# A decoder trunk on one core: the first layer's modulation and norm, done by halves in another order

## The chip, the core and the metric

The kernel runs on one core of a Trainium2 chip. The metric is device time in microseconds (us) of one launch. Engines, as the profile names them: PE is TensorE (PEld its weight loads), DVE is VectorE, ACT is ScalarE, POOL is GpSimd, SP is SyncE, which issues the large DMA transfers here.

## The reference

A trunk of two layers over 256 tokens of width 1024, float32. Each layer has three sub-layers (a half-step SwiGLU feed-forward network, FFN; a mixer; a second FFN), each behind an RMSNorm that is modulated by a vector computed from `c`. What the change touches is the start: the modulation of the very first norm, that norm, and the first products of the first FFN.

```python
def rmsnorm(x, g):
    y = xf * lax.rsqrt(jnp.mean(xf * xf, axis=-1, keepdims=True) + EPS)
    return y * g
def modulated_norm(x, g, shift, scale):
    return rmsnorm(x, g) * (1 + scale) + shift
def swiglu(h, wg, wu, wd):
    return (jax.nn.silu(h @ wg) * (h @ wu)) @ wd
c_act = jax.nn.silu(c)
mod = (c_act @ w_ada[l] + b_ada[l]).reshape(b, N_MOD, 1, D_MODEL)
sh1, sc1, g1, sh2, sc2, g2, sh3, sc3, g3 = [mod[:, i] for i in range(N_MOD)]
h = modulated_norm(x, norm_g[l, 0], sh1, sc1)
x = x + 0.5 * g1 * swiglu(h, ffn_wg[l, 0], ffn_wu[l, 0], ffn_wd[l, 0])
```

## The kernel before

**Layout.** Activations lie transposed: eight tiles `xt[t]` of 128 features by 256 tokens. Weights come from memory in float32; each weight tile is split into a high part `wh` (ACT, L369) and a low part `wl` (DVE or POOL, L384), and each activation tile into `hi` and `lo`. A product is three matmuls, wh·hi, wl·hi and wh·lo, one after the other for every 128 features (`mm`, L306 to L317).

**The start.** SP loads `x`, then the columns of `w_ada` that give shift and scale. These come in two halves: half 0 for features 0 to 511, half 1 for features 512 to 1023, each as eight loads of 512 KB. One such load holds 128 of the 1024 rows of `w_ada` (every eighth), 512 scale and 512 shift columns; the code calls the k-th load row k. For a half, DVE adds up the eight rows, each times its value of silu(c), into one tile `acc0` (L159 for the first row, L161 for the others), and PE sums over the 128 partitions with eight matmuls against a column of ones (L1390). DVE adds the bias and makes the factor `gsc` and the shift (L1396, L1399).

Meanwhile PE transposes `x`, ACT copies the results to `xt` and squares them, POOL adds up the squares (L1487), PE sums them over partitions (L564), and the reciprocal root is computed by small operations, nearly all of them on POOL (L448 to L456). The result is spread over the partitions by PE (L582) into `rtile`; POOL multiplies `xt` by it (L590), and DVE, POOL and ACT make hi and lo of the normalized tiles (L609, L610, L614).

**The first products.** Before the second half of the normalized tiles exists, the FFN can begin on the first: `lead` makes units. A unit is two blocks of 128 FFN columns over one half of the features, 24 matmuls. Six unit pairs (`LEADS = 12` blocks of columns) run on half 0: five, then the products of half 1's modulation, then the sixth; then the same six run on half 1. After these the FFN goes on with whole columns (`plain`: one block, all features, also 24 matmuls).

**What sets the order.** The program order is written step by step (`Step`, `run`, `plan`): before a step's matmuls, `split_high` and `split_low` issue the splits of later steps up to a lead time. `hold` shifts this time for a step, and `LLO` names the engine of the low split in the units. At most `UBUF = 5` split weight tiles are live. Raw weights and the rows of `w_ada` share a ring of `RAWB = 8` buffers of 1 MB: a load waits until the buffer's last user is done, and SP issues in order, so a waiting load holds up all behind it. The rest of the modulation (128 rows) is added up by DVE in the background at a rate per step (`tick`, `MTICK`).

## Time and profile before

| | |
|---|---|
| time, median of 3 runs | 1019.17 us (1018.66 to 1019.98) |
| profiled execution | 1018.38 us, of which its span is 1016.6 us |
| busy in the span | PE 96%, DVE 79%, ACT 48%, POOL 4% |
| TensorE's clock over the span | 0.985 of full |

The span runs from the first to the last instruction. 96% is an average: the idle time and the time at the lower clock lie at the two ends, and the stretch from 0 to 89 us is the one to read closely. Matmul ends are modelled, so a row's duration covers one matmul's whole passage; the pace is the distance between starts.

### The profile page before, as it was taken

To read this page: it belongs to the slowest core of one execution; us is meant where nothing else is said; L and a number is where in the kernel's file an instruction comes from. 1 tells how busy PE (TensorE), PEld (TensorE's weight loads), DVE (VectorE), ACT (ScalarE), POOL (GpSimd) and SP (SyncE) were. 2 spreads that over 40 slices of the span, in tenths; PEclk is the share of its full clock that TensorE was granted. 3 is DMA by queue.
4 is the path that set the end of the run, shared out by engine and by line. 5 is a ranking of instruction groups with operands and counts; after the bars stand their busy time and mean duration, and the time that the engine had idled before them with its cause. 6 is when DMAs were issued, how large, how long until landed. Compare 5 with 4: busy or idle time off the path is not lost.

```text
span 1016.6 us, 17795 instructions
## 1 busy us (share of the span) xinstructions
PE 972.2 (96%) x7126; PEld 919.1 (90%) x7126; DVE 801.3 (79%) x1288; ACT 483.3 (48%) x841; POOL 45.7 (4%) x81
## 2 busy tenths in 40 slices
PE   3879999999999899999999999999999999999998
PEld 1879999889878799999889999988999999999986
DVE  4768888888988799999898988888688889555552
ACT  2435444444653555444555544444564456444441
POOL 6820000000000000000000000000000000000000
PEclk9779999999999899999999999999999999999999
DMA  9879998888617659998796899876645556645410
GB/s 356 307 268 321 332 312 282 284 295 309 224 43 250 231 176 366 323 372 308 277 329 227 260 336 318 301 242 201 208 165 191 183 167 210 204 157 168 144 52 22
DMA packets 183284, 247.05 MB, mean 243 GB/s; under 512 B 5968, under 2 KB 156548, under 8 KB 183200
## 3 DMA queue, kind: packets, MB, share of 16 engines
q1 hardware_dynamic: 182944, 245.78, 70.2%
q8 instruction: 56, 0.92, 0.3%
q14 instruction: 28, 0.23, 0.1%
q0 software_dynamic: 256, 0.12, 0.0%
HBM read 244.84 MB, written 1.05 MB: 242 GB/s over the span
## 4 chain that ended last, share of the span: by engine, by line
PE 69%; DVE 21%; ACT 4%; issue 2%; DMA 2%; POOL 1%; SPq 0%; ACTq 0%; DVEq 0%; POOLq 0%
PE pu L315 45%; PE acc L326 11%; DVE wl L384 7%; PE acc L327 6%; DVE acc L161 4%; PE acc L315 3%; DVE nh L600 1%; DVE xp L605 1%; ACT wh L369 1%; PE acc L995 1%; DMA raw<-in_ffn_wg_dram 1%; DVE tx L628 1%; DMA raw<-in_ffn_wu_dram 1%; PE pu L1390 1%; POOL ssum L1487 1%
## 5 line engine op out<-in xcount | busy, mean ns | idle before, releaser
L315 PE MATMUL pu<-xp,wh 128*128 128x256 f32 (+1 forms) x3008 | 547.4, 283 | 6.2 <-DVE xp L530 2.6
L315 PEld LDWEIGHTS pu<-xp,wh 128*128 128x128 f32 x3008 | 467.0, 190 | 8.4 <-DVE xp L530 3.1
L315 PE MATMUL pu<-xp,wl 128*128 128x256 f32 (+1 forms) x1504 | 423.7, 282 | 0.7 <-DVE wl L384 0.7
L384 DVE TENSOR_TENSOR wl<-raw,wh 128x1024 fp32r<-128x1024 f32 (+1 forms) x315 | 375.5, 1202 | 17.7 <-ACT wh L369 17.5
L369 ACT CAST wh<-raw 128x1024 fp32r<-128x1024 f32 (+1 forms) x320 | 325.6, 1026 | 78.5 <-PE acc L326 33.7
L315 PEld LDWEIGHTS pu<-xp,wl 128*128 128x128 f32 x1504 | 286.0, 190 | 0.9 <-DVE wl L384 0.9
L326 PE MATMUL acc<-a,wh 128*128 128x512 f32 x448 | 160.7, 400 | 0.0
L161 DVE SCALAR_TENSOR_TENSOR acc<-adaw,cact,acc 128x1024 f32<-128x1024 f32 x119 | 151.9, 1276 | 0.4
L327 PE MATMUL acc<-a,wl 128*128 128x256 f32 x448 | 125.9, 281 | 0.0
L326 PEld LDWEIGHTS acc<-a,wh 128*128 128x128 f32 x448 | 84.2, 188 | 20.0
L326 PE MATMUL acc<-xp,wh 128*128 128x512 f32 x256 | 91.6, 397 | 0.0
L327 PEld LDWEIGHTS acc<-a,wl 128*128 128x128 f32 x448 | 84.7, 189 | 0.0
L824 DVE TENSOR_TENSOR pu<-pu,sg 128x256 f32<-128x256 f32 x72 | 30.8, 428 | 61.2 <-PE pu L315 61.1
L327 PE MATMUL acc<-xp,wl 128*128 128x256 f32 x256 | 71.6, 280 | 0.0
L816 ACT ACTIVATE sg<-pu 128x256 f32<-128x256 f32 x66 | 25.2, 385 | 77.9 <-PE pu L315 77.9
L315 PE MATMUL acc<-xp,wh 128*128 128x258 f32 (+1 forms) x288 | 56.6, 293 | 3.1 <-ACT xp L610 3.1
L326 PEld LDWEIGHTS acc<-xp,wh 128*128 128x128 f32 x256 | 48.1, 188 | 11.8
L315 PEld LDWEIGHTS acc<-xp,wh 128*128 128x128 f32 x288 | 47.3, 198 | 3.4 <-ACT xp L610 3.2
L327 PEld LDWEIGHTS acc<-xp,wl 128*128 128x128 f32 x256 | 48.3, 189 | 0.0
L692 DVE SCALAR_TENSOR_TENSOR u<-acc,hg,xt 128x256 f32<-128x256 f32 x32 | 15.4, 481 | 40.7 <-PE acc L327 40.6
L333 ACT CAST a<-pu 128x256 fp32r<-128x256 f32 x40 | 14.9, 374 | 66.3 <-DVE pu L824 66.3
L315 PE MATMUL acc<-xp,wl 128*128 128x258 f32 (+1 forms) x144 | 41.7, 289 | 0.0
(199 smaller groups left out, 815.9 us busy)
## 6 DMA issues: line engine op xcount, KB each, us to landing
adaw<-in_w_ada_dram SPq DMA_DIRECT2D x128, 512.0 KB, 5.4
raw<-in_ffn_wg_dram SPq DMA_DIRECT2D x44, 1024.0 KB, 5.6
raw<-in_ffn_wu_dram SPq DMA_DIRECT2D x44, 1024.0 KB, 5.4
raw<-in_ffn_wd_dram SPq DMA_DIRECT2D x32, 1024.0 KB, 6.9
raw<-in_ffn_wd_dram SPq DMA_DIRECT2D x16, 768.0 KB, 5.7
raw<-in_w_in_c_dram SPq DMA_DIRECT2D x12, 1024.0 KB, 5.2
raw<-in_w_ada_dram SPq DMA_DIRECT2D x16, 512.0 KB, 10.4
raw<-in_w_in_ab_dram SPq DMA_DIRECT2D x8, 1024.0 KB, 7.8
```

What stands on the lines that cost most here:

```text
L161: nc.vector.scalar_tensor_tensor(out=acc, in0=w, scalar=scales[:, k:k + 1], in1=acc, op0=ALU.mult, op1=ALU.add)
L315: nc.tensor.matmul(ps, lhsT=a[:, k, :], rhs=m, start=start and i == 0, stop=stop and i == n - 1, skip_group_check=True)
L326: nc.tensor.matmul(both, lhsT=wh[:, i, :], rhs=x, start=start and i == 0, stop=False, skip_group_check=True)
L327: nc.tensor.matmul(bank_[:, 0:T], lhsT=wl[:, i, :], rhs=x[:, 0, :], start=False, stop=stop and i == len(ks) - 1, skip_group_check=True)
L333: nc.scalar.copy(hi, src)
L369: nc.scalar.copy(shaped(hi, r), r)
L384: eng.tensor_tensor(out=shaped(lo, r), in0=r, in1=shaped(hi, r).bitcast(F32), op=ALU.subtract)
L600: nc.vector.scalar_tensor_tensor(out=h, in0=xt[t], scalar=g, in1=rtile[:, 0:T], op0=ALU.mult, op1=ALU.mult)
L605: nc.vector.scalar_tensor_tensor(out=lo, in0=h, scalar=s, in1=hi.bitcast(F32), op0=ALU.add, op1=ALU.subtract)
L692: nc.vector.scalar_tensor_tensor(out=u, in0=b, scalar=g, in1=r, op0=ALU.mult, op1=ALU.add)
L816: nc.scalar.activation(out=s, in_=v, func=AF.Silu)
L824: nc.vector.tensor_tensor(out=v, in0=v, in1=s, op=ALU.mult)
```

## The change

- **Squares.** ACT squares `x` as it was loaded (tokens on partitions), two operations over 1024 columns whose accumulator gives the sum of each token. The eight squares of `xt`, POOL's seven additions and PE's two sums (L564) go. The reciprocal root and its broadcast are computed by DVE, as for the later norms.
- **Rows shared.** Of half 0's eight rows, PE takes rows 2, 4 and 6 directly: eight matmuls each with the row's weights against silu(c), repeated over 64 columns (`WIDE`), accumulating in PSUM. DVE adds up rows 0, 1, 3, 5 and 7 in `acc0`, and PE adds that last, in the same PSUM banks. Half 1's rows all stay with DVE.
- **Norm.** The normalized tiles are made as in the later norms: one DVE operation (xt·gsc·rtile), ACT for `hi`, DVE for `lo`. POOL has no arithmetic left at the start. Factor and shift of half 0 come in two pieces of two tiles each.
- **Units.** Seven unit pairs instead of six run on half 0; half 1's products stand between the sixth and the seventh. All low splits are DVE's. The unit's weights are loaded as 512 KB of two blocks instead of 1 MB of four. Half 1's rows are spread over DVE's order ahead of units 3, 4 and 5 (`FIRST`), where they stood in one run ahead of the sixth. The first unit does all its wh matmuls ahead of its wl matmuls.
- **Warm-up.** Eleven matmuls of the identity stand ahead of the transposes, where two of 512 columns stood ahead of the spread.

```diff
-WARM = 2
-MIDP = 5
+WARM, WIDE = 11, 64
-LEADS = 12
-MIDC, LHOLD, LPOOL = 0, (-0.5, 5.0), (2,)
-LLO = (("pool", "pool", "vector", "pool", "vector", "pool"), ...
+LEADS = 14
+FIRST = {3: range(0, 2), 4: range(2, 5), 5: range(5, 8)}
+LHOLD = 5.0
+PEROWS = (2, 4, 6)
-RTICK, MTICK = 0.0, (0.75, 0.6, 0.6, 0.6)
+RTICK, MTICK = 0.0, (0.82, 0.6, 0.6, 0.6)
...
-            for which, f0 in ((0, 0), (1, 0), (0, 4)):
-                halves[which, f0] = [Load((wg, wu)[which][4 * h * P:4 * (h + 1) * P, f0 * P:(f0 + 4) * P], 4, 4 * P)
+            pairs = [(0, 0), (0, 2), (1, 0), (1, 2), (0, 4), (0, 6), (1, 4)]
+            for which, f0 in pairs:
+                halves[which, f0] = [Load((wg, wu)[which][4 * h * P:4 * (h + 1) * P, f0 * P:(f0 + 2) * P], 4, 2 * P)
                                      for h in range(2)]
...
+                todo = [(k, u, a, m) for k in range(4) for u in range(2) for a, m in ((wh, 0), (wh, 1), (wl, 0))]
+                if h == 0 and j == 0:
+                    todo.sort(key=lambda v: v[2] is wl)
...
+            if h == 0 and j // 2 in FIRST:
+                s.enter = lambda: start_macs(1, FIRST[j // 2])
         for j in range(0, LEADS, 2):
-            if j == 2 * MIDP:
-                add(Step(start_mods[1], ticks=0, enter=lambda: start_macs[1](range(KT)), post=start_tiles[1], cost=MIDC))
+            if j == LEADS - 2:
+                add(Step(lambda: start_row(1, None), ticks=0, post=start_second, cost=0))
             unit(0, j)
...
+    def start_row(h, k, ts=range(4)):
...
+        w, m = (wa[KT * h + k], cact[:, k:k + 1]) if k is not None else (box0["acc", h], ones[:, 0:1])
...
+                nc.tensor.matmul(pt[:, 2 * (t % per) + v, :], lhsT=w[:, 512 * v + t * P:512 * v + (t + 1) * P],
+                                 rhs=m.to_broadcast([P, WIDE]), start=box0["n", h][b] == 0,
+                                 stop=k is None and v == 0 and t % per == per - 1, skip_group_check=True)
...
-    wu = bank(ps_u, "pu")
-    for n in range(WARM):
-        nc.tensor.matmul(wu, lhsT=xr[1][:, 0:P], rhs=xr[1][:, 0:512], start=True, stop=True)
...
+    for _ in range(WARM):
+        nc.tensor.matmul(wu[:, 0:P], lhsT=ident, rhs=ident, start=True, stop=True)
+    for i in range(2):
+        nc.scalar.activation(out=junk, in_=xr[i], func=AF.Square, accum_out=norm.pr[:, i:i + 1])
+    start_macs(0, range(1))
...
+    norm.chain()
+    start_row(0, 2)
+    norm.spread()
+    nc.scalar.copy(rtile[:, 0:T], norm.pb[:, 0:T])
+    start_macs(0, range(1, 4))
+    start_row(0, 4)
+    start_macs(0, range(4, 6))
+    start_row(0, 6)
+    start_macs(0, range(6, KT))
+    for b in range(2):
+        start_row(0, None, range(2 * b, 2 * b + 2))
```

**DVE, half 1's rows.** In the kernel before, DVE's order from the last low part of half 0's normalized tiles to the factor of half 1. `raw` as an input of L159 or L161 is a row of `w_ada`, `wl` a low split of a unit's weights.

```order
L614 TENSOR_TENSOR xp_301<-nh_302,xp_301 128x256
L384 TENSOR_TENSOR wl_317<-raw_136,wh_309 128x1024
L384 TENSOR_TENSOR wl_356<-raw_138,wh_313 128x1024
L159 TENSOR_SCALAR acc_88_472<-raw_140,cact 128x1024
L161 SCALAR_TENSOR_TENSOR acc_88_472<-raw_140,cact,acc_88_472 128x1024
L161 SCALAR_TENSOR_TENSOR acc_88_472<-raw_143,cact,acc_88_472 128x1024 x2
L161 SCALAR_TENSOR_TENSOR acc_88_472<-raw_146,cact,acc_88_472 128x1024 x2
L161 SCALAR_TENSOR_TENSOR acc_88_472<-raw_149,cact,acc_88_472 128x1024 x2
L384 TENSOR_TENSOR wl_483<-raw_152,wh_445 128x1024
L1396 TENSOR_TENSOR mod_270<-pu_485,params 128x4
```

The same stretch of DVE's order in the changed kernel, where L587 is the low part of a normalized tile and L1374 and L1376 add up the rows:

```order
L587 SCALAR_TENSOR_TENSOR xp_316<-nh_317,mod_294,xp_316 128x256
L384 TENSOR_TENSOR wl_322<-raw_134,wh_291 128x1024
L384 TENSOR_TENSOR wl_328<-raw_136,wh_324 128x1024
L384 TENSOR_TENSOR wl_357<-raw_138,wh_326 128x1024
L384 TENSOR_TENSOR wl_386<-raw_140,wh_355 128x1024
L1374 TENSOR_SCALAR acc_69_413<-raw_148,cact 128x1024
L1376 SCALAR_TENSOR_TENSOR acc_69_413<-raw_148,cact,acc_69_413 128x1024
L384 TENSOR_TENSOR wl_418<-raw_142,wh_384 128x1024
L1376 SCALAR_TENSOR_TENSOR acc_69_413<-raw_151,cact,acc_69_413 128x1024 x2
L1376 SCALAR_TENSOR_TENSOR acc_69_413<-raw_154,cact,acc_69_413 128x1024
L384 TENSOR_TENSOR wl_450<-raw_144,wh_416 128x1024
L1376 SCALAR_TENSOR_TENSOR acc_69_413<-raw_154,cact,acc_69_413 128x1024
```

Two low splits stood ahead of the rows before; now four stand ahead of the first row and six ahead of the last. Two more row operations follow, then the last splits.

**SP, the loads.** In the kernel before, from the last rows of half 0 to the first weights of half 1:

```order
L1434 DMA raw_131<-in_w_ada_dram 128x2x512 x2
L281 DMA raw_134<-in_ffn_wg_dram 128x4x512
L281 DMA raw_136<-in_ffn_wu_dram 128x4x512
L281 DMA raw_138<-in_ffn_wg_dram 128x4x512
L1434 DMA raw_140<-in_w_ada_dram 128x2x512 x2
L1434 DMA raw_143<-in_w_ada_dram 128x2x512 x2
```

In the changed kernel, from the same place:

```order
L1432 DMA raw_131<-in_w_ada_dram 128x2x512 x2
L281 DMA raw_134<-in_ffn_wg_dram 128x4x256
L281 DMA raw_136<-in_ffn_wg_dram 128x4x256
L281 DMA raw_138<-in_ffn_wu_dram 128x4x256
L281 DMA raw_140<-in_ffn_wu_dram 128x4x256
L281 DMA raw_142<-in_ffn_wg_dram 128x4x256
L281 DMA raw_144<-in_ffn_wg_dram 128x4x256
L281 DMA raw_146<-in_ffn_wu_dram 128x4x256
L1432 DMA raw_148<-in_w_ada_dram 128x2x512 x2
L1432 DMA raw_151<-in_w_ada_dram 128x2x512 x2
```

Seven loads of 512 KB stand where three of 1 MB stood, each in a buffer of its own, so half 1's rows reuse other buffers: `raw_148` that of half 0's rows 6 and 7, `raw_151`, `raw_154` and `raw_157` those of the first three units' weights.

## Rows read from the trace of the kernel before

**Rows 1.** Page, TensorE's granted clock in 40 slices of 25.4 us, tenths.

```profile
PEclk9779999999999899999999999999999999999999
```

**Rows 2.** Stretches: length; busy of PE, PEld, DVE, ACT, POOL; clock, DMA share, GB/s.

```profile
0.00:34.20 34.20, 14.02 (x45) 9.15 (x45) 13.74 (x14) 10.19 (x27) 23.04 (x39) 0.88 0.98 370
27.70:31.10 3.40, 3.40 (x17) 3.31 (x16) 0.00 (x0) 1.32 (x2) 2.72 (x4) 0.50 1.05 408
34.20:40.00 5.80, 5.78 (x26) 5.63 (x27) 4.38 (x7) 5.22 (x7) 3.48 (x3) 0.50 0.47 184
40.00:51.40 11.40, 11.36 (x96) 11.16 (x95) 11.26 (x7) 3.15 (x3) 11.40 (x6) 1.00 0.89 285
51.40:57.00 5.60, 0.00 (x0) 0.00 (x0) 5.49 (x5) 0.00 (x0) 0.53 (x1) 0.70 1.06 365
60.50:64.00 3.50, 3.50 (x18) 3.50 (x19) 3.23 (x11) 2.91 (x5) 0.69 (x1) 0.52 0.65 231
88.80:194.70 105.90, 105.52 (x842) 102.90 (x841) 90.97 (x116) 48.25 (x76) 0.00 (x0) 1.00 0.89 305
```

**Rows 3.** PE's waits, 0 to 120 us: total, times, longest.

```profile
PE misc L564 <- POOL ssum L1487: 7.1, 1, 7.1
...
PE pu L1390 <- DVE acc L161: 5.7, 1, 5.7
```

**Rows 4.** DVE in time order, half 0's rows: start, duration, instructions [idle before].

```profile
8.17 0.75 DVE L159 TENSOR_SCALAR acc<-raw,cact 128x1024 f32<-128x1024 f32 x1 [8.17 <-DMA raw<-in_w_ada_dram]
9.42 6.28 DVE L161 SCALAR_TENSOR_TENSOR acc<-raw,cact,acc 128x1024 f32<-128x1024 f32 x4 [0.49 <-DMA raw<-in_w_ada_dram]
...
19.36 3.92 DVE L161 SCALAR_TENSOR_TENSOR acc<-raw,cact,acc 128x1024 f32<-128x1024 f32 x3
```

**Rows 5.** PE in time order, the products and the first unit.

```profile
27.68 3.41 PE L1390 MATMUL pu<-ones,acc 128*128 128x1 f32 x16
34.22 0.58 PE L315 MATMUL acc<-xp,wh 128*128 128x256 f32 x1 [3.12 <-ACT xp L610]
...
35.67 0.63 PE L315 MATMUL acc<-xp,wh 128*128 128x256 f32 x2
...
36.31 0.63 PE L315 MATMUL acc<-xp,wh 128*128 128x256 f32 x2
```

**Rows 6.** DVE in time order, half 1's rows and splits.

```profile
37.56 5.92 DVE L384 TENSOR_TENSOR wl<-raw,wh 128x1024 fp32r<-128x1024 f32 x2 [1.42 <-ACT wh L369]
...
44.67 12.30 DVE L161 SCALAR_TENSOR_TENSOR acc<-raw,cact,acc 128x1024 f32<-128x1024 f32 x7
```

**Rows 7.** DVE in time order, up columns 4 and 5 taken up.

```profile
86.02 0.43 DVE L824 TENSOR_TENSOR pu<-pu,sg 128x256 f32<-128x256 f32 x1 [0.74 <-PE pu L315]
...
88.86 0.43 DVE L824 TENSOR_TENSOR pu<-pu,sg 128x256 f32<-128x256 f32 x1 [0.95 <-PE pu L315]
```

**Rows 8.** DVE groups after 200 us: count, busy us, mean ns.

```profile
L384 DVE TENSOR_TENSOR wl<-raw,wh 128x1024 fp32r<-128x1024 f32 x236 | 285.0, 1217 | 10.4 <-ACT wh L369 10.2
L161 DVE SCALAR_TENSOR_TENSOR acc<-adaw,cact,acc 128x1024 f32<-128x1024 f32 x92 | 117.5, 1277 | 0.4
...
L600 DVE SCALAR_TENSOR_TENSOR nh<-xt,gsc,rtile 128x256 f32<-128x256 f32 x40 | 17.8, 477 | 0.0
```

**Rows 9.** DVE in time order, a later norm's reciprocal root, first and last line.

```profile
246.42 0.15 DVE L467 TENSOR_SCALAR var<-misc 128x2 f32<-128x2 f32 x1
...
248.78 0.48 DVE L576 TENSOR_SCALAR yb<-ones,rs_y 128x128 f32<-128x128 f32 x2
```

**Rows 10.** ACT groups of the whole span: count, busy us, mean ns.

```profile
L369 ACT CAST wh<-raw 128x1024 fp32r<-128x1024 f32 x288 | 300.3, 1048 | 64.5 <-PE pu L315 22.2 <-PE acc L326 19.7 <-issue 13.0
...
L601 ACT ACTIVATE xp<-nh,mod 128x256 fp32r<-128x256 f32 x40 | 18.5, 499 | 0.9 <-DVE nh L600 0.9
```

**Rows 11.** Stretches with rows of w_ada alone (first), FFN weights alone (second).

```profile
12.00:18.00 6.00, 0.07 (x1) 0.07 (x1) 3.63 (x3) 0.74 (x3) 5.57 (x5) 1.00 1.05 408
54.00:58.00 4.00, 0.97 (x5) 0.97 (x5) 3.93 (x4) 0.00 (x0) 0.00 (x0) 0.50 1.07 373
```

More of the change, by code (lines that the diff above doesn't have):

```diff
@@ L567, in chain @@
         def chain(self):
-            y = mean_rsqrt(self.pr[:, 0:2], 2, D, self.start)
+            y = mean_rsqrt(self.pr[:, 0:2], 2, D)
             still[0] = False
@@ L572, in chain @@
                 yb = scr.tile([P, P], F32, name=nm("yb"), tag="yb")
-                if self.start:
-                    nc.scalar.activation(out=yb, in_=ones, func=AF.Copy, scale=y[:, i:i + 1])
-                else:
-                    nc.vector.tensor_scalar(out=yb, in0=ones, scalar1=y[:, i:i + 1], scalar2=None, op0=ALU.mult)
+                nc.vector.tensor_scalar(out=yb, in0=ones, scalar1=y[:, i:i + 1], scalar2=None, op0=ALU.mult)
                 self.yb.append(yb)
@@ L841, in ffn @@
         if norm.start:
-            head = [(0, f) for f in range(4)] + [(1, f) for f in range(4)] + [(0, f) for f in range(4, 8)]
+            head = [(which, f0 + u) for which, f0 in pairs for u in range(2)]
             first_step = lead(norm, halves, (gate_out, up_out), head)
-            order = [(1, f) for f in range(4, 8)]
+            order = [(1, f) for f in range(6, 8)]
         else:
@@ L878, in pe @@
                     accs[j] = bank(ps_a, "acc") if j < 8 else bank(ps_u, "pu")
-                hs = norm.hs[4 * h:4 * h + 4]
-                for k in range(4):
-                    for u in range(2):
-                        wu = [a[:, :, u * P:(u + 1) * P] for a in w]
-                        mm(accs[j][:, u * T:(u + 1) * T], wu, hs, h == 0 and k == 0 and u == 0, h == 1 and k == 3, [k])
+                hs, acc = norm.hs[4 * h:4 * h + 4], accs[j]
+                wh, wl = w
+                todo = [(k, u, a, m) for k in range(4) for u in range(2) for a, m in ((wh, 0), (wh, 1), (wl, 0))]
+                if h == 0 and j == 0:
+                    todo.sort(key=lambda v: v[2] is wl)
+                for i, (k, u, a, m) in enumerate(todo):
+                    nc.tensor.matmul(acc[:, u * T:(u + 1) * T], lhsT=a[:, k, u * P:(u + 1) * P], rhs=hs[k][m],
+                                     start=h == 0 and i == 0, stop=h == 1 and k == 3 and a is wl, skip_group_check=True)
             def post():
                 if h == 0:
-                    start_extra.get(j, tuple)()
                     return ()
@@ new lines, in start_macs @@
+    def start_macs(h, ks):
+        for k in ks:
+            if k in box0.get(("pe", h), ()):
+                continue
+            first = ("acc", h) not in box0
+            if first:
+                box0["acc", h] = box0["pool"].tile([P, D], F32, name=nm("acc0"))
+            acc, w = box0["acc", h], wa[KT * h + k]
+            if first:
+                nc.vector.tensor_scalar(out=acc, in0=w, scalar1=cact[:, k:k + 1], scalar2=None, op0=ALU.mult)
+            else:
+                nc.vector.scalar_tensor_tensor(out=acc, in0=w, scalar=cact[:, k:k + 1], in1=acc, op0=ALU.mult, op1=ALU.add)
@@ new lines, in start_vectors @@
+    def start_vectors(h, b):
+        norm = norms[0]
+        if norm.gsc is None:
+            norm.gsc = const.tile([P, KT], F32, name=nm("gsc"))
+            mods.update(((0, i), const.tile([P, KT], F32, name=nm("mod"))) for i in range(2))
+            norm.sh = mods[0, 0]
+        per = 4 if h else 2
+        t0 = 4 * h + per * b
+        pt, ks = box0["pt", h][b].rearrange("p (t v n) -> p t v n", v=2, n=WIDE), slice(t0, t0 + per)
+        for v in (1, 0):
+            nc.vector.tensor_tensor(out=mods[0, v][:, ks], in0=pt[:, 0:per, v, 0],
+                                    in1=params[:, v * KT + t0:v * KT + t0 + per], op=ALU.add)
+        g0 = NOFF + t0
+        nc.vector.scalar_tensor_tensor(out=norm.gsc[:, ks], in0=mods[0, 1][:, ks], scalar=1.0,
+                                       in1=params[:, g0:g0 + per], op0=ALU.add, op1=ALU.mult)
@@ L1413, in trunk, with start_tiles, start_second @@
+    def start_tiles(ts, lows=()):
+        lows = list(lows)
+        for t in ts:
+            low = norms[0].tile(t)
+            if lows:
+                lows.pop(0)()
+            lows.append(low)
+        return lows
+    def start_second():
+        start_vectors(1, 0)
+        for f in start_tiles(range(4, KT)):
+            f()
+        return ()
     ffn(0, 0, norms[0], norms[1], enter=schedule(0, RATES[0]))
@@ L1459, in trunk @@
         param_load(0)
-    start_extra[X0] = lambda: xn.extend(norm.scaled(t, sp) for t in range(4, KT))
     start_extra["params"] = [(X1 + i, lambda: param_load(1)) for i in range(5)] + [(X1 + X2, lambda: param_turn(1))]
```

124 lines of the change are left out of this document (35 added, 89 removed).

## The prediction

> **What bounds the kernel now.** I read the clock by slices first [rows 1]: TensorE is below full speed only in the slices around 25 to 76 us and once more near 340 us. The busy time by stretch says the rest: from 88.8 to 194.7 us PE is busy 105.5 of 105.9 us at full clock, while in the first 34.2 us it is busy for 14 [rows 2]. So PE's matmuls bound the kernel as soon as they run, and the change is worth what it moves the time at which the same matmuls are done. My mark is the end of up column 5, the 14th block of columns of the first FFN: up to it both kernels do 336 matmuls. DVE takes that block up at 88.86 us [rows 7], so PE is done with it at 88.75. Up columns 4 and 5 are 2.84 us apart, which is PE's pace at full clock: 24 matmuls, 0.118 us each. At 1.2 GHz, where the granted clock is 0.50, three matmuls take 36.31 − 35.67 = 0.64 us [rows 5], 0.213 each.
>
> 336 matmuls at 0.118 us take 39.8 us. The other 49 of the 88.75 us are: 34.2 us until the first of them [rows 5]; 5.7 us in which PE waits for DVE's sum of half 1's rows [rows 3]; 3.4 us for the products of half 1, if they take as long as those of half 0 [rows 5]; and the lower clock from 34.2 to 40.0 us (26 matmuls) and from 60.5 to 64 us (18) [rows 2], 44 × 0.095 = 4.2 us. The remaining 1.5 us are small waits.
>
> **What goes, step by step.** *Up to the first matmul.* Before, a chain on POOL ends last: PE waits 7.1 us for POOL's additions of the squares [rows 3], and the root, the products and the tiles follow. Now the root is DVE's; from its first to its last operation it took 249.26 − 246.42 = 2.84 us in a later norm [rows 9]. The squares are two ACT operations of 1024 columns, about 1.05 us each like the casts [rows 10]; `x` is loaded ahead of the rows of `w_ada`, so they lie beside row 0, which DVE ends at 8.92 us [rows 4]. I put the root at 11.8 us. Each row of 512 KB lands 1.285 us after the one ahead at 408 GB/s [rows 11] (rows 0 and 1 were taken up 1.25 apart, each after a wait for its DMA [rows 4]), so row 7 lands at 9.42 + 6 × 1.285 = 17.1 us. DVE has rows 1, 3, 5 and 7 left, 1.28 us each [rows 8]; the last ends at 18.5, where the sum ended at 23.3 before [rows 4]. The root costs nothing, since the landing of row 7 covers it. It would cost its 2.8 us if DVE had all eight rows: two of the three given to PE are what hides it.
>
> Then come PE's eight products, the first four of them for the first bank. Before, eight took 3.41 us at 1.2 GHz with one column [rows 2, 5]. For 64 columns there is no row; I bound it by 1.7 us (the same at 2.4 GHz) and 3.4 us, and take the lower, because eleven matmuls and sixteen transposes now stand ahead. So the first bank is ready at 19.4; three small DVE operations (0.4 us), one of 0.48 [rows 8] and ACT's 0.50 [rows 10] give the first `hi`: first matmul at 21.1 us. The four tiles are eight DVE operations about 0.43 us apart and a second set of small ones, to 24.2 us; the first low split follows, to 25.4; the first unit, whose wl matmuls stand last, ends at 26.4. DVE and ACT feed it, so its clock hardly matters.
>
> *Half 1's rows.* From 24.2 us DVE has six splits of 1.15 us (mean 1.217, overlapping a little [rows 8]), 6.9 us, one row of 0.75 [rows 4] and seven of 1.30, 9.9 us: 41.0 us. Before, two splits took 5.92 us and seven rows 12.30 [rows 6], with POOL busy throughout [rows 2]; now POOL is idle. The rows land in time: first seven 512 KB loads of weights at 373 GB/s [rows 11], 1.41 us each, then eight rows of 1.285, from 17.1 us on: 37.3 for the last, 38 with the release of its buffer, and DVE wants it at 39.7. PE meanwhile: 26.4 + 5 units × 2.84 = 40.6 us. Both meet at 41, and the wait of 5.7 us is nearly gone. The products at full clock take 1.75: 42.8. DVE makes half 1's tiles while PE does the seventh unit, so the second stop for tiles is covered too.
>
> A rule speaks against the loads: the Trainium skill, "DMA: Bandwidth & Descriptors", section "Bandwidth", wants transfers batched to at least 1 MiB, as smaller ones reach less of the bandwidth. [...] This trace disagrees as far as it goes: 512 KB rows land 1.25 us apart with several in flight.
>
> *To the mark.* One unit of half 0 and seven of half 1, 8 × 2.84 = 22.7: 65.5 us. For hops between engines that no row shows, and for part of the lower clock, I add 1.5 us: 67.0. The gain at the mark is 88.75 − 67.0 = 21.7 us.
>
> *Behind the mark.* Nothing is taken away there, and every engine's order is the same from the middle of the first FFN's down projection on. Two fewer steps carry background rows, which the larger `MTICK` makes up. DVE was at 91.0 of 105.9 us beside a full PE [rows 2], so the shift should stay whole. DMA's share of 0.89 there hides the loads as long as the buffer ring is full, which it can be: at 67 us all of half 1's weights have landed for 15 us.
>
> **Sum.** 1018.38 − 21.7 = 996.7 us for the profiled execution; the median of the runs lies 0.8 above that execution: 997.5 us.
>
> **The rivals.** *Lower clock until half 1's products.* After PE stood still from 51.4 to 57 us it ran at 1.2 GHz until about 64, through some 6 us of work [rows 2]. If warm-up, transposes and row products don't hold the clock up, PE itself is late at the start: rows 2, 4, 6 and the sum take 3.4 us each and the spread 1.2, from 10.7 us on, so the products end at 25.5 instead of 20.3 us. DVE's wait catches a little of it: mark at 69.8, gain 19.0, 1000.2 us. For it: the products with one column ran wholly at the lower clock [rows 2]. Against it: PE now has work nearly without a break ahead of them.
>
> *Half loads that cost like whole ones,* the mechanism beside the rule above: 2.57 us instead of 1.41 for each of seven, so half 1's last row lands at 46 us, its sum ends at 47 instead of 41, and the mark moves by 5 to 6: gain 16.5, about 1002.5 us. The 512 KB rows speak against it.
>
> *The shift is given back later.* If DVE at 86% or DMA at 89% [rows 2] were only just enough, PE would wait for splits behind the mark. Before, PE is idle 0.4 us in those 105.9; half the gain lost would be much, 1008 us.
>
> *Slower.* TensorE could stay at 1.2 GHz through all units, if the small waits between them keep the clock down. Price: 336 × 0.095 = 32 us, and 5 for the products ahead: mark at 102, 13 us later than before, 1032 us. It decides from 21.7 / 0.095 = 230 slow matmuls on; before, 44 were slow, so this is remote.
>
> *No effect.* Something as late as 34.2 us would have to hold the first matmul, a load above all. The sum follows the loads at the rate they have, and I see nothing.
>
> **How the numbers follow.** Forecast (gain 19.5 to 25, the best with no small waits and the clock up from the start) 0.72; lower clock before the products 0.13; half loads 0.07; given back later 0.05; slower 0.015; no change 0.015. The measurement tells about 0.2% (2 us) from no change. The range goes from the forecast's best, 993.5, to the half loads' 1002.5, and leaves out the last three and the tails. Faster by over 0.2%: 0.97; same 0.01; slower 0.02.
>
> **What would show it.** In the profile after: the first unit's matmul at 21 to 22 us (near 25 with the lower clock); half 1's products near 41 with under 1 us of wait ahead; splits of 1.2 and rows of 1.28 us on DVE throughout; up column 5 taken up near 67; the same lengths behind it. It is wrong if half 1's rows land after 40 us, if the units run at 0.21 us a matmul, or if PE begins to wait for `wl` behind the mark.

## The result and the profile after

The changed kernel takes **999.97 us** (median; 997.96 to 1002.77), the kernel before 1019.58 us (1018.66 to 1020.09) beside it: ratio **0.9814**, 95% interval 0.9803 to 0.9826. The profiled execution took 1000.42 us, its span 998.6. So the kernel is faster by 19.6 us, inside the range, and 2.5 us short of the forecast of 997.5. Its runs lie 4.8 us apart, those of the kernel before 1.4.

The page of the kernel after, busy time by engine and the granted clock in 40 slices; compare [rows 1]:

```profile
PE 976.1 (98%) x7188; PEld 926.5 (93%) x7188; DVE 797.2 (80%) x1309; ACT 481.4 (48%) x834; POOL 7.6 (1%) x45
...
PEclk7999999999999899999999999999999999999999
```

PE's waits from 0 to 110 us (total, times, longest), all of them:

```profile
PE misc L1477 <- POOL ident masks.py:199: 1.4, 1, 1.4
PE acc L1359 <- DMA raw<-in_w_ada_dram: 1.3, 1, 1.3
PE pu L1486 <- ACT xt L1487: 0.7, 1, 0.7
```

The two waits of [rows 3], 7.1 us for POOL's sum and 5.7 us for DVE's, are gone, and from 12.5 us on PE waits for nothing up to 110 us. PE in time order at the start (start, duration, instructions):

```profile
9.20 0.32 PE L1452 MATMUL pu<-ident,rows 120*128 120x120 f32 x1
10.86 2.21 PE L1359 MATMUL acc<-cact,raw 128*128 128x64 f32 x16 [1.35 <-DMA raw<-in_w_ada_dram]
12.87 1.17 PE L570 MATMUL misc<-ident,yb 128*128 128x128 f32 x4
13.83 6.93 PE L1359 MATMUL acc<-cact,raw 128*128 128x64 f32 x32
20.55 3.62 PE L1359 MATMUL acc<-ones,acc 128*128 128x64 f32 x16
24.11 1.10 PE L859 MATMUL acc<-xp,wh 128*128 128x256 f32 x2
...
44.34 1.89 PE L1359 MATMUL misc<-ones,acc 128*128 128x64 f32 x16
46.03 0.48 PE L859 MATMUL pu<-xp,wh 128*128 128x256 f32 x2
```

Row 2 takes 2.2 us, rows 4 and 6 and the final products 3.5 and 3.6 us each, and half 1's products, the same 16 matmuls, 1.89. (The trace counts each of these float32 products twice: x16 are the eight products of a row.) The stretches show the clock that they ran at: length; busy time of PE, PEld, DVE, ACT, POOL; clock, DMA share, GB/s.

```profile
5.70:12.50 6.80, 4.70 (x36) 3.60 (x34) 4.15 (x17) 4.10 (x14) 0.31 (x1) 1.00 1.06 398
12.50:24.10 11.60, 11.60 (x56) 11.48 (x54) 5.29 (x10) 1.97 (x4) 0.00 (x0) 0.50 1.07 391
24.10:29.60 5.50, 5.50 (x22) 4.77 (x22) 5.25 (x12) 4.15 (x7) 0.00 (x0) 0.50 0.90 328
29.60:44.30 14.70, 14.70 (x125) 14.70 (x125) 14.52 (x14) 5.12 (x6) 0.00 (x0) 1.00 1.03 363
```

TensorE is at 2.4 GHz until 12.5 us, with gaps (busy 4.70 of 6.80 us from 5.7 us on), and then at 1.2 GHz until 29.6 us, though it works without a break all that time. It is the late engine here, and DVE waits for it. DVE in time order, to be read beside [rows 4, 6]:

```profile
11.41 2.60 DVE L1376 SCALAR_TENSOR_TENSOR acc<-raw,cact,acc 128x1024 f32<-128x1024 f32 x2
...
17.33 1.29 DVE L1376 SCALAR_TENSOR_TENSOR acc<-raw,cact,acc 128x1024 f32<-128x1024 f32 x1 [1.27 <-DMA raw<-in_w_ada_dram]
22.57 0.23 DVE L1389 TENSOR_TENSOR mod<-acc,params 128x2 f32<-128x2 f32 x2 [3.95 <-PE acc L1359]
...
27.26 4.62 DVE L384 TENSOR_TENSOR wl<-raw,wh 128x1024 fp32r<-128x1024 f32 x4
...
34.92 3.92 DVE L1376 SCALAR_TENSOR_TENSOR acc<-raw,cact,acc 128x1024 f32<-128x1024 f32 x3
...
39.89 3.92 DVE L1376 SCALAR_TENSOR_TENSOR acc<-raw,cact,acc 128x1024 f32<-128x1024 f32 x3
43.73 2.35 DVE L384 TENSOR_TENSOR wl<-raw,wh 128x1024 fp32r<-128x1024 f32 x2
```

DVE's sum ends at 18.62, then DVE waits 3.95 us for PE's products. Splits take 1.15 us and rows 1.3 throughout, where they took 2.96 and, on average, 1.76 before [rows 6]. The average mixes three kinds. In the kernel before a row took 1.65 us beside GpSimd's multiplications, 3.28 beside its split and 1.3 after GpSimd had stopped at 51.9 us; DVE, then POOL:

```profile
44.67 1.65 DVE L161 SCALAR_TENSOR_TENSOR acc<-raw,cact,acc 128x1024 f32<-128x1024 f32 x1
...
49.73 3.28 DVE L161 SCALAR_TENSOR_TENSOR acc<-raw,cact,acc 128x1024 f32<-128x1024 f32 x1
...
53.05 2.61 DVE L161 SCALAR_TENSOR_TENSOR acc<-raw,cact,acc 128x1024 f32<-128x1024 f32 x2
```

```profile
48.57 3.36 POOL L384 TENSOR_TENSOR wl<-raw,wh 128x1024 fp32r<-128x1024 f32 x1
```

**Where the lead goes.** I call lead the time by which a place in the program comes sooner than in the profile of before. The 336th matmul of the units ends at 68.98 us where it ended at about 88.75: lead 19.8. At the root behind the down projection it is 20.35 (226.07 us, before 246.42 [rows 9]) and at the attention's third root 20.31. At its fourth, 18.29. DVE there, before and after:

```profile
312.59 6.56 DVE L161 SCALAR_TENSOR_TENSOR acc<-adaw,cact,acc 128x1024 f32<-128x1024 f32 x5
...
319.07 0.16 DVE L467 TENSOR_SCALAR var<-sso 128x4 f32<-128x4 f32 x1
```

```profile
292.28 6.56 DVE L161 SCALAR_TENSOR_TENSOR acc<-adaw,cact,acc 128x1024 f32<-128x1024 f32 x5
...
299.58 1.28 DVE L161 SCALAR_TENSOR_TENSOR acc<-adaw,cact,acc 128x1024 f32<-128x1024 f32 x1 [0.73 <-DMA adaw<-in_w_ada_dram]
300.78 0.16 DVE L467 TENSOR_SCALAR var<-sso 128x4 f32<-128x4 f32 x1
```

And PE behind it, after:

```profile
301.01 0.63 PE L188 MATMUL misc<-ident,acc 128*128 128x128 f32 x4 [1.28 <-DVE var L467]
```

Before, DVE does five background rows ahead of that root, now six, and the sixth waits 0.73 us for its load: 2.0 us. Nothing more of size follows: the lead is 18.2 at the next norm (329.20, before 347.40) and 18.0 at the end.

### The profile page after: what moved, and what is told of

Its sections match the earlier page's. It is cut to its first block, busy times and chain, and to the rows that moved or that the text cites. A ratio compares the mean times of both kernels' runs of the same rounds, so it can differ in the third digit from the quotient of the medians.

```text
span 998.6 us, 17893 instructions
## 1 busy us (share of the span) xinstructions
PE 976.1 (98%) x7188; PEld 926.5 (93%) x7188; DVE 797.2 (80%) x1309; ACT 481.4 (48%) x834; POOL 7.6 (1%) x45
## 4 chain that ended last, share of the span: by engine, by line
PE 75%; DVE 16%; DMA 3%; ACT 3%; issue 2%; SPq 0%; ACTq 0%; DVEq 0%
PE pu L315 45%; PE acc L326 11%; PE acc L327 6%; DVE wl L384 5%; PE acc L972 3%; DVE acc L161 3%; PE acc L859 3%; PE acc L315 3%; PE pu L859 2%; PE acc L1359 1%; DVE nh L582 1%; DVE xp L587 1%; DMA raw<-in_w_ada_dram 1%; DMA raw<-in_ffn_wg_dram 1%; DMA raw<-in_ffn_wu_dram 1%
## 5 line engine op out<-in xcount | busy, mean ns | idle before, releaser
L315 PE MATMUL pu<-xp,wh 128*128 128x256 f32 (+1 forms) x2912 | 528.4, 283 | 5.9 <-DVE xp L521 2.9
L315 PEld LDWEIGHTS pu<-xp,wh 128*128 128x128 f32 x2912 | 451.6, 190 | 8.0 <-DVE xp L521 3.4
L315 PE MATMUL pu<-xp,wl 128*128 128x256 f32 (+1 forms) x1456 | 410.0, 282 | 0.0
L315 PEld LDWEIGHTS pu<-xp,wl 128*128 128x128 f32 x1456 | 276.5, 190 | 0.0
L161 DVE SCALAR_TENSOR_TENSOR acc<-adaw,cact,acc 128x1024 f32<-128x1024 f32 x119 | 152.1, 1278 | 1.1 <-DMA adaw<-in_w_ada_dram 0.7
L326 PEld LDWEIGHTS acc<-a,wh 128*128 128x128 f32 x448 | 84.2, 188 | 19.8
L326 PEld LDWEIGHTS acc<-xp,wh 128*128 128x128 f32 x256 | 48.1, 188 | 11.6
L498 ACT ACTIVATE xp<-acc,gsc 128x256 fp32r<-128x256 f32 x24 | 11.4, 474 | 65.9 <-DVE acc L668 61.6
L333 ACT CAST xp<-pu 128x256 fp32r<-128x256 f32 x32 | 11.9, 373 | 60.5 <-DVE pu L798 60.5
L315 PE MATMUL acc<-xp,wh 128*128 128x258 f32 x160 | 30.9, 286 | 0.0
```

The source lines that it names most:

```text
L161: nc.vector.scalar_tensor_tensor(out=acc, in0=w, scalar=scales[:, k:k + 1], in1=acc, op0=ALU.mult, op1=ALU.add)
L315: nc.tensor.matmul(ps, lhsT=a[:, k, :], rhs=m, start=start and i == 0, stop=stop and i == n - 1, skip_group_check=True)
L326: nc.tensor.matmul(both, lhsT=wh[:, i, :], rhs=x, start=start and i == 0, stop=False, skip_group_check=True)
L333: nc.scalar.copy(hi, src)
```

## The experiments

The table gives the lead in each profile, in us, at six places: the end of the 336th matmul, the root behind the down projection (246.42 before), the attention's third and fourth root (307.83, 319.07), the next norm (347.40), and the span's end. Beside it the start of the first unit's matmul, the median of the runs and the ratio to the runs of before on the same chip.

| kernel | first unit | 336th | down | third | fourth | next | end | median | ratio, interval |
|---|---|---|---|---|---|---|---|---|---|
| changed | 24.11 | 19.8 | 20.35 | 20.31 | 18.29 | 18.20 | 18.0 | 999.97 | 0.9814, 0.9803–0.9826 |
| e4_dve | 28.68 | 10.0 | 10.02 | 9.95 | 9.93 | 9.84 | 10.0 | 1009.52 | 0.9901, 0.9887–0.9914 |
| e8_norows | 24.46 | 19.7 | 20.18 | 20.11 | 17.91 | 17.41 | 17.6 | 1001.34 | 0.9828, 0.9815–0.9842 |
| e10_wide | 22.26 | 21.9 | 22.41 | 22.34 | 19.69 | 19.62 | 19.9 | 999.56 | 0.9805, 0.9789–0.9820 |
| e3_rows24 | 22.18 | 21.3 | 21.85 | 21.83 | 19.62 | 18.06 | 18.2 | 999.19 | 0.9800, 0.9787–0.9814 |
| e2_fill | 21.78 | 22.2 | 22.68 | 22.61 | 20.17 | 20.08 | 20.1 | 998.21 | 0.9793, 0.9780–0.9807 |
| e2_again | 21.68 | 22.1 | 22.65 | 21.76 | 19.27 | 19.17 | 18.9 | 998.55 | 0.9796, 0.9783–0.9810 |
| e7_six | 21.99 | 19.6 | 19.58 | 19.53 | 19.53 | 19.43 | 20.0 | 1000.99 | 0.9819, 0.9804–0.9833 |
| e1_tick | 21.90 | 22.2 | 21.12 | 20.24 | 20.22 | 20.12 | 20.3 | 1000.45 | 0.9809, 0.9795–0.9822 |
| e6_rate | 23.93 | 19.8 | 18.65 | 17.19 | 17.19 | 17.08 | 17.2 | 1001.17 | 0.9825, 0.9812–0.9839 |
| e5_best | 22.47 | 21.7 | 20.57 | 18.28 | 18.29 | 18.30 | 18.4 | 1000.17 | 0.9814, 0.9798–0.9830 |
| e11_best2 | 21.69 | 22.2 | 20.24 | 19.96 | 18.60 | 17.72 | 17.3 | 1001.24 | 0.9827, 0.9812–0.9842 |
| e9_skip | 23.80 | 20.0 | 20.58 | 20.51 | 20.48 | 18.55 | 18.2 | 1000.42 | 0.9815, 0.9801–0.9828 |

A profile shows one start of several: e1, e6 and e9 have the changed kernel's start unaltered, and their clocks fell at 16.5, 12.7 and 12.3 us, the first units at 21.90, 23.93 and 23.80. So differences between first units below 2.2 us tell nothing, and of medians of the scattering kernels none below about 1.5 us; within one profile the lead's course tells. The profiled executions of e1 (998.09 us) and e7 (998.45) are the fastest of their sets by 2.3 us and more, so their leads at the end stand above what their medians say.

### How much is GpSimd's part?

**e4_dve**: the kernel before, with the work that GpSimd shares with VectorE given to VectorE. GpSimd keeps the sum of squares and the multiplication by the root.

```diff
-MIDC, LHOLD, LPOOL = 0, (-0.5, 5.0), (2,)
-LLO = (("pool", "pool", "vector", "pool", "vector", "pool"), ("vector", "vector", "vector", "vector", "pool", "vector"))
+MIDC, LHOLD, LPOOL = 0, (-0.5, 5.0), ()
+LLO = (("vector",) * 6, ("vector",) * 6)
...
-            y = mean_rsqrt(self.pr[:, 0:2], 2, D, self.start)
+            y = mean_rsqrt(self.pr[:, 0:2], 2, D)
```

> The kernel before with one part of the change alone: the reciprocal root and all low splits of the units and the normalized tiles' scaling go from GpSimd to VectorE; GpSimd keeps the additions of the squares and the multiplication by the root. Theory (GpSimd's slow operations and the slowing of VectorE beside it made up about half of the gain): first unit's matmul at 30 to 31 us instead of 34.2, half 1's rows 1.3 us each instead of 1.76, half 1's products at about 48 instead of 57 us, mark (up column 5) 8 to 10 us earlier, time about 1010. Rival (what counts is the order, rows shared with TensorE and spread among the splits): under 3 us of gain, since VectorE has three more splits ahead of the rows.

DVE's rows and splits of half 1, in time order:

```profile
32.88 5.75 DVE L384 TENSOR_TENSOR wl<-raw,wh 128x1024 fp32r<-128x1024 f32 x5
...
39.34 9.21 DVE L161 SCALAR_TENSOR_TENSOR acc<-raw,cact,acc 128x1024 f32<-128x1024 f32 x7
```

Half of the gain comes from taking this work off GpSimd alone: 10.0 us at the 336th matmul, and it stays whole to the end. Splits are 1.15 and rows 1.32 us as in the changed kernel, although the same engine now has more of them. The lead of 10.0 us is not lost anywhere behind, so whatever eats the changed kernel's is no law of the later stages.

### Is TensorE the late engine at the start, and by its clock?

**e2_fill**, run again as **e2_again** beside other kernels: 16 more small matmuls on the identity, into a bank that nobody reads, where TensorE has gaps (the fills, below).

```diff
+    fb = bank(ps_u, "pu")
+
+    def fill(n):
+        for _ in range(n):
+            nc.tensor.matmul(fb[:, 0:P], lhsT=ident, rhs=ident, start=True, stop=True)
     norm.chain()
+    fill(6)
     start_row(0, 2)
     norm.spread()
+    fill(2)
     nc.scalar.copy(rtile[:, 0:T], norm.pb[:, 0:T])
     start_macs(0, range(1, 4))
     start_row(0, 4)
+    fill(4)
     start_macs(0, range(4, 6))
     start_row(0, 6)
+    fill(4)
```

> The changed kernel with 16 more identity matmuls (128 columns) on TensorE at the start, where it waited or would wait at full clock: 6 ahead of row 2, 2 behind the spread, 4 behind row 4, 4 behind row 6. Theory (the clock fell at 12.5 us because TensorE had stood still or worked little since 7 us, and the row products then ran at 1.2 GHz and made TensorE late): granted clock 1.00 from about 6 us into the units, the row products take 1.8 us instead of 3.5, first unit's matmul at 21 to 22 us instead of 24.1, up column 5 taken up about 2.5 us earlier, time about 997.5, and the runs lie closer together. Rival (the row products don't hold the clock whatever stands between them): clock 0.50 again, the added matmuls cost 0.43 us each there, first unit's matmul at 26 to 29 us, time 1002 to 1004.

> The same kernel as e2_fill, beside the others on one chip. Theory: the identity matmuls keep the clock up from 6.6 us on and the runs agree among themselves again: 998.2 us, within 1.5 us of each other, ratio 0.979. Rival: its 1.8 us below the changed kernel were the chance of those four runs: 1000 us, spread over 4 us like the changed kernel.

Stretches of e2_fill, columns as above:

```profile
6.60:21.80 15.20, 13.81 (x118) 12.81 (x116) 9.46 (x26) 5.55 (x16) 0.00 (x0) 1.00 1.07 396
...
23.70:27.10 3.40, 3.40 (x15) 3.01 (x15) 3.22 (x5) 3.12 (x4) 0.00 (x0) 0.50 1.08 394
27.10:44.00 16.90, 16.90 (x145) 16.90 (x145) 16.52 (x17) 5.28 (x6) 0.00 (x0) 1.00 1.07 395
```

More work made the start shorter than in the changed kernel's profile. The clock stays at 2.4 GHz from 6.6 to 23.7 us, the row products take 1.9 us each, and the first unit starts at 21.78, 2.3 us sooner; the lead at the 336th matmul is 2.4 us longer. The nine runs of the two sets lie between 997.76 and 999.61, where the changed kernel's four span 4.8 us. In e2_again's profile the clock stayed up from 4.8 us right through the start. The narrow spread alone shows little: e6 and e9, with the changed kernel's start, span 0.7 and 1.1 us, and e11, with these fills, 2.5.

The start of e1, which is the changed kernel's unaltered, shows what the clock is worth without any fill. There the clock fell at 16.5 us, so rows 2 and 4 took 2.0 us each. PE in time order, rows 4 and 6 and the final products:

```profile
12.99 2.00 PE L1359 MATMUL acc<-cact,raw 128*128 128x64 f32 x16
15.56 2.85 PE L1359 MATMUL acc<-cact,raw 128*128 128x64 f32 x16 [0.57 <-DMA raw<-in_w_ada_dram]
18.32 3.64 PE L1359 MATMUL acc<-ones,acc 128*128 128x64 f32 x16
```

DVE's sum ends at 18.17 there, so TensorE is late by 0.15 us, not by the 1.9 of the changed kernel's profile, and its lead at the 336th matmul is 22.2 us, that of e2. TensorE is the late engine in the executions whose clock falls early, not in all; against a late fall the fills bring 0.1 us.

**e3_rows24**: row 6 goes back to VectorE.

```diff
-PEROWS = (2, 4, 6)
+PEROWS = (2, 4)
...
-    start_row(0, 6)
```

> The changed kernel with rows 2 and 4 alone on TensorE; DVE adds up row 6 too. DVE's last row is bound by its load (row 7 lands at about 17.3 us), and row 6 fits ahead of it, so the sum on DVE ends at 18.6 us as it did. Theory (TensorE, at the lower clock, is the late engine at the start: its rows end at 20.5 us): without row 6 the last products start at 18.7 instead of 20.55 us, first unit's matmul near 22.3 instead of 24.1, time about 998.3. Rival (DVE is the late engine, and the third row was worth taking from it): DVE's sum and the first matmul 1.3 us later, time 1001.

PE in time order:

```profile
18.59 3.65 PE L1359 MATMUL acc<-ones,acc 128*128 128x64 f32 x16 [3.42 <-DVE acc L1376]
22.18 4.48 PE L859 MATMUL acc<-xp,wh 128*128 128x256 f32 x16
```

DVE's sum ends at 18.44 with six rows as it does at 18.62 with five: row 7 lands no sooner, and the third row on TensorE bought nothing. With it gone, TensorE waits 3.42 us for the sum and is not late: the final products start with the sum, and the first unit is 1.9 us sooner than in the changed kernel's profile, though the products still run at 1.2 GHz (this profile's clock fell at 18.3 us). By itself that difference tells nothing, since e1 reached 21.90 with all three rows on TensorE. The median, 999.19, does not tell the two apart.

**e8_norows**: all of half 0's rows on VectorE.

```diff
-PEROWS = (2, 4, 6)
+PEROWS = ()
...
-    start_row(0, 2)
...
-    start_row(0, 4)
...
-    start_row(0, 6)
```

> The changed kernel with all eight rows of half 0 on VectorE (TensorE's three are taken from it). Theory: TensorE is the late engine at the start, not VectorE: VectorE's sum then ends at about 20.5 us (seven rows of 1.3 us behind the root at 11.4) instead of 18.6, TensorE comes to the final products idle and does them in 3.6 us at 1.2 GHz, so that the first unit starts at 24.1 to 24.6 as in the changed kernel (24.1): 1000.0 us, between 999 and 1001.5. Rival: sharing the rows is what brings the start forward, as the prediction had it; three rows more on VectorE make the start 3.9 us later: 1003.9 us.

```profile
20.88 3.65 PE L1359 MATMUL acc<-ones,acc 128*128 128x64 f32 x16 [8.69 <-DVE acc L1376]
24.46 4.48 PE L859 MATMUL acc<-xp,wh 128*128 128x256 f32 x16
```

PE, in the same view, stands idle for 8.69 us and still starts its first unit at 24.46, 0.35 us behind the changed kernel's profile. What three rows on TensorE save on VectorE, TensorE loses again where its clock falls at 12.5 us. Against the starts whose clock fell later (21.90 in e1, 21.99 in e7) the three rows are worth 2.5 us. The time lies in the theory's range, and the rival's 1003.9 outside the interval; the medians of this kernel and the changed one can't be told apart.

**e10_wide**: of each half's seven half loads, the first six joined into three of 1 MiB.

```diff
-            for which, f0 in pairs:
-                halves[which, f0] = [Load((wg, wu)[which][4 * h * P:4 * (h + 1) * P, f0 * P:(f0 + 2) * P], 4, 2 * P)
+            slabs = [(0, 0, 4), (1, 0, 4), (0, 4, 4), (1, 4, 2)]
+            for which, f0, n in slabs:
+                halves[which, f0] = [Load((wg, wu)[which][4 * h * P:4 * (h + 1) * P, f0 * P:(f0 + n) * P], 4, n * P)
...
```

> The changed kernel with its first three pairs of half loads joined again to loads of 1 MiB (the seventh pair keeps its half load). Theory: the size of the loads is not where the gain is; the first slab lands 1.3 us later, at about 20 us instead of 18.65, is split by 21 us, and the first unit starts at 24.1 us anyway: 1000.0 us, between 999 and 1001.5. Rival: the halves bring the first slab sooner on the path that sets the start: 1001.3 us or more, with the first unit at 25.4.

ACT's first cast, which waits for the first slab:

```profile
19.77 1.04 ACT L369 CAST wh<-raw 128x1024 fp32r<-128x1024 f32 x1 [6.07 <-DMA raw<-in_ffn_wg_dram]
```

The slab lands at 19.77 us instead of 18.65, still ahead of its use at 22.26. With 999.56 us the size of the loads brings nothing and costs nothing that can be measured. The first unit comes at 22.26, not at the 24.1 expected, and that is the clock again, which fell at 17.0 us here. From 18 to 22 us the joined loads moved 409 GB/s, the half loads of the changed kernel 385: larger loads were 6% faster, far from the factor of 1.8 (2.57 against 1.41 us) that the prediction's rival needed.

### What do seven unit pairs bring?

**e7_six**: six pairs, half 1's rows one unit sooner, `MTICK` back at 0.75, so that the background's rows stand as before the change.

```diff
-LEADS = 14
-FIRST = {3: range(0, 2), 4: range(2, 5), 5: range(5, 8)}
+LEADS = 12
+FIRST = {2: range(0, 2), 3: range(2, 5), 4: range(5, 8)}
...
-RTICK, MTICK = 0.0, (0.82, 0.6, 0.6, 0.6)
+RTICK, MTICK = 0.0, (0.75, 0.6, 0.6, 0.6)
...
-            pairs = [(0, 0), (0, 2), (1, 0), (1, 2), (0, 4), (0, 6), (1, 4)]
+            pairs = [(0, 0), (0, 2), (1, 0), (1, 2), (0, 4), (0, 6)]
...
```

> The changed kernel with six unit pairs on the first half instead of seven (half 1's rows one unit earlier in VectorE's order, the background as before the change). Theory: TensorE is late at the start and busy without a gap until half 1's products at 44.3 us, while VectorE's rows for them end at 43.8; with five units ahead of the products instead of six TensorE comes there at about 41.5, one split less leaves VectorE there at 42.6, so TensorE waits 1 to 2.5 us. The lead at the end of the down projection is then 18 to 19.3 us instead of 20.3, and it stays so through the attention, since the background is the old one: 999.3 us, between 998.2 and 1001. Rival: the seventh pair covers nothing that VectorE would not have reached in time: the lead stays 20.3 us to the end, 998.0 us.

PE at half 1's products:

```profile
40.62 2.00 PE L1359 MATMUL misc<-ones,acc 128*128 128x64 f32 x16 [0.96 <-DVE acc L1376]
```

Against e1_tick, whose first unit started at the same time (21.90 and 21.99), the seventh pair is worth 2.6 us at the 336th matmul (22.2 and 19.6), 0.96 of it this wait and 0.54 a wait for a low split at 60.6 us. But e7's lead then stays whole to the end, within 0.4 us, and e1's loses 2 us. At the end they are 0.3 us apart, and the medians cannot be told apart. Nearly all that the seventh pair brings is given back.

### Why is it given back?

With seven pairs, two fewer steps of the up columns carry background rows, and one row more is left for later. All kernels that leave the background as changed show what it costs: e2, e2_again, e3, e8 and e10 lose 2.2 to 2.7 us between the third and the fourth root, where e4 and e7, with the background of before, lose nothing. Four kernels put the row in other places, and a fifth leaves it out.

**e1_tick**:

```diff
-RTICK, MTICK = 0.0, (0.82, 0.6, 0.6, 0.6)
+RTICK, MTICK = 0.0, (0.86, 0.6, 0.6, 0.6)
```

> The changed kernel with the rate of background rows in the first FFN's down projection at 0.86 a step instead of 0.82; everything else as changed. The order then agrees with that of the kernel before from the down projection on, so the attention has 5 background rows ahead of its transposes of the sum, as before, not 6. Theory (the sixth row, with its wait for a load, cost 2.05 us there): the distance between the two kernels stays the same through the attention, some 20.3 us from the second norm on; the time falls by 2.0 us to about 998. Rival (those 2 us are DMA or clock chance of the one profile, not the order): the attention takes the 2 us again, time as changed, 1000.

PE's waits, 150 to 252 us, the first:

```profile
PE misc L188 <- DVE acc L161: 1.6, 1, 1.6
```

The attention now loses nothing (20.24, 20.22), as the theory has it, but the row stands directly ahead of a modulation's transposes in the down projection, and TensorE waits 1.6 us for it there. The median is unchanged, as the rival has it: three of the four runs took 1000.4 to 1000.6 us.

**e6_rate**: the changed kernel with `RATES[0]` at (0, 0.83) instead of (0, 0.8).

> The changed kernel with the background's rate at 0.83 and nothing else. Theory: the 2.05 us lost in the attention are the sixth background row that VectorE does there; the higher rate puts it into the steps of the up matrices, where VectorE has time, and none stands directly ahead of a modulation's product (in e1_tick one did, and TensorE waited 1.6 us for it). The lead of 20.3 us at the end of the down projection is kept to the end, TensorE's waits on L161 are at most 0.3 us in all: 998.0 us, between 997 and 999 (the start's clock moves it by 1 us either way). Rival: the row's time comes back elsewhere, as in e1_tick: 1000.0 us.

PE's waits from 150 to 262 us, and a stretch behind them:

```profile
PE pu L315 <- ACT xp L498: 1.2, 1, 1.2
PE misc L555 <- DVE ssum L512: 0.8, 1, 0.8
PE pu L315 <- DVE wl L384: 0.3, 1, 0.3
```

```profile
227.70:231.20 3.50, 3.50 (x19) 3.50 (x19) 3.12 (x17) 1.52 (x2) 0.00 (x0) 0.51 0.80 224
```

The row goes from the attention (17.19, 17.19), but at the end of the down projection PE waits 1.2 us for an `xp` of ACT's, which itself waits for DVE's update ahead of it (L668), and behind these waits TensorE's clock is at 1.2 GHz for 3.5 us, which neither the kernel before nor the changed one shows there. The lead falls to 17.2, and the time, 1001.17, is above the rival's 1000.0.

**e5_best** (the fills, 20 of them behind row 4 and four behind the products; row 6 on VectorE; the rate of 0.83) and **e11_best2** (the fills of e2; rate 0.81, `MTICK[0]` 0.90) were meant to keep e2's start and lose nothing behind it.

> The changed kernel with three edits: small identity matmuls between TensorE's row products as in the run e2_fill (20 behind row 4 and 4 behind the final products), row 6 given back to VectorE, and the background's rate at 0.83 instead of 0.80, so that the attention has five background rows again and none stands directly ahead of a modulation's product. Theory: row 6 on TensorE buys nothing, since VectorE waits 1.27 us for row 7 to land anyway; the final products then start with VectorE's sum at 18.5 and at full clock take 1.9 us, the first unit starts at 21.2 or a little sooner (21.78 in e2_fill), and the lead at the end of the first feed-forward (22.7 us in e2_fill) is kept through the attention. Time 996.0 us, between 995.0 and 997.2. Rival: the background row costs its 2 us wherever it is put, as in the run e1_tick: lead at the end 20 us, 998 us.

> The changed kernel with the identity matmuls of e2_fill and the background at rate 0.81 and 0.90 per step of the down projection, so that four rows instead of six are left to the attention, none stands directly ahead of a modulation's product, and the last one ahead of the norm's root stands where it stood before the change. Theory: the start of e2_fill (lead 23.1 us at the up columns' end) is kept but for 1 us at most of VectorE's rows in the down projection, and the attention loses nothing: lead 22 to 23 us at the end, 995.7 us, between 995 and 997.5. Rival: VectorE has no room for a row more ahead of the norm, wherever it stands; TensorE waits for it there as in e1_tick, e5_best and e6_rate, and the lead at the end is 20 us: 998.3 us.

Both fail, and with 1000.17 and 1001.24 us by more than their rivals say. The lead of 21.7 and 22.2 us at the 336th matmul is 20.57 and 20.24 behind the down projection, and 18.4 and 17.3 at the end. As in e6 the clock falls there: 0.79 on average from 223 to 231 us in e5 and from 224 to 232 in e11, where the changed kernel has 1.00. In e11, though only four rows are left to the attention, PE waits there for the last of them (at 298 us); its waits from 150 to 335 us have the line:

```profile
PE misc L188 <- DVE acc L161: 2.1, 1, 2.1
```

**e9_skip**: the sixth row of the attention is left out, its load stays.

```diff
-            ada_mac(acc, fetched.pop(0)[1], r, cact if n == 1 else cact2)
+            w = fetched.pop(0)[1]
+            if not (group[0] == (0, 6) and r == 15):
+                ada_mac(acc, w, r, cact if n == 1 else cact2)
```

> The changed kernel without one background row: the last of the sixteen of the modulation pair that VectorE finishes in the attention is left out (its load stays), so this kernel leaves out a part of one modulation. All else stands in the same order. Theory: the 2.05 us lost in the attention are that row (1.3 us, and the 0.73 us that VectorE waits for its load), at the one place where VectorE has nothing ahead of TensorE: the lead of 20.3 us at the end of the down projection is kept to the end, TensorE's wait for var there goes from 1.3 us to nothing, 998.0 us (997.0 to 999.0). Rival: the loss has another cause in the attention (its own order of steps, another clock): it stays 18.3 us, 1000.0 us.

DVE in the attention and behind it:

```profile
298.59 0.16 DVE L469 TENSOR_SCALAR var<-sso 128x4 f32<-128x4 f32 x1
...
305.86 1.28 DVE L161 SCALAR_TENSOR_TENSOR acc<-adaw,cact,acc 128x1024 f32<-128x1024 f32 x1 [2.69 <-DMA adaw<-in_w_ada_dram]
```

In the attention the theory holds: 20.51 and 20.48, and no wait for `var`. Yet the time is 1000.42. The next group's second row lands so late that DVE waits 2.69 us for it; the lead is 18.55 at the next norm. In e1, which did the row sooner, the same operation starts at 303.48 without a wait, and SP had one load of a row less to issue in this stretch. SP in e9 and, below it, in e1:

```profile
297.35 10.36 SPq L224 DMA_DIRECT2D adaw<-in_w_ada_dram  x5
```

```profile
297.62 7.70 SPq L222 DMA_DIRECT2D adaw<-in_w_ada_dram  x4
```

So VectorE's time for the row is only a part of it. The load that was left in has taken its turn among the loads, and it must be done sooner as well as the row. That is read from the two traces; no run takes the load away alone.

## Why the prediction came out as it did

**Right in its steps.** The squares and the root are off the path; DVE's sum ends at 18.62 (forecast 18.5); rows and splits on DVE are 1.3 and 1.15 us without GpSimd; from DVE's first low split to its last row of half 1 it took 27.26 to 43.8 us, 16.5, where the forecast had 24.2 to 41.0, 16.8; half 1's products wait for nothing; eight units from them to the mark take 46.03 to 68.98, 22.95 us (forecast 22.7). The half loads cost what they should: at the 385 GB/s of 18 to 22 us one takes 1.36 us, an estimate from that rate (forecast 1.41). The Trainium skill, "DMA: Bandwidth & Descriptors", section "Bandwidth", wants batches of at least 1 MiB. This trace differs, with 391 GB/s from 12.5 to 24.1 us on loads of 512 KB, and e10 gained nothing measurable by the larger ones. One reading was wrong: POOL was not busy throughout half 1's rows. By [rows 2] it was busy 0.53 of 5.60 us from 51.4 us on, and DVE's rows took 1.3 us there already.

**Wrong: the products' clock.** The step that failed is the choice of the lower price, 1.7 us, for the eight products, "because eleven matmuls and sixteen transposes now stand ahead". The clock was up to 12.5 us only; rows 4 and 6 and the products ran at 1.2 GHz, 3.5 to 3.6 us each, TensorE came to the products 1.9 us behind DVE's sum, and the first unit started at 24.1 instead of 21.1. That is the first rival, lower clock until half 1's products, in its mechanism, though the clock was back at 29.6 us, ahead of those. The forecast's 1.5 us for small waits and clock was more than was needed, so at the mark 2.0 of the 3.0 us are left: 69.0, between the forecast's 67.0 and that rival's 69.8. That the time comes out beside that rival's 1000.2 is chance: half of what is missing went later, by a mechanism that it hadn't. With the clock up the products do take 1.9 us (e2, first unit at 21.8).

**Wrong: "which the larger `MTICK` makes up".** It doesn't: one background row was left over, and it costs 2.0 us in the attention. The third rival, the shift is given back later, is this mechanism at a fifth of the 10.8 us it had there, though PE waits for a norm's root and not for splits. I looked at DVE's busy share behind the mark (91.0 of 105.9 us) and took it for room. The runs show that there is none where it counts: e1, e5, e6 and e11 moved the row ahead and lost 1.1 to 2.0 us in the down projection, where PE waits 1.6 us for the row itself (e1) or 1.2 us for the `xp` behind it (e5, e6, e11).

**The sum.** Of a forecast lead of 21.7 us 1.9 are missing at the mark; 0.6 come in up to the down projection's end; 2.1 go from there to the attention's fourth root and 0.3 behind it: 18.0, against 17.96 between the two profiled executions (1018.38 and 1000.42). The forecast for the profiled execution, 996.7, is 3.7 us off, that for the median 2.5, since the profiled one is among the slower of runs that scatter with the clock: the mean granted clock was 0.990 and 0.991 in the two faster runs and 0.986 in the two slower. The range's lower end, 993.5, is 1018.38 less 25 without the 0.8 us that the other times carry.

**What stays open.** Which place would take the row for nothing: none of four was one, and fewer loads in flight were not tried. Why e3 loses 1.6 us more between the attention's fourth root and the next norm wasn't taken apart. Why the clock fell at 12.5 us in one run and at 16.5 in another of the same start isn't shown by any row.

The fastest kernel here is e2_fill, 998.2 and 998.6 us in two sets, 0.2% below the changed kernel, with intervals that still touch.
